# Recurrence chunks worked two heads at a time, and sparse scores as three 64-row products a head

## The chip, the cores and the metric

The kernel runs on one core of a Trainium2 chip, in one launch. The metric is the device time of that core in microseconds (us), the median of several executions. All arithmetic stands in the kernel; the host only lays out the arrays.

## What is computed

One forward pass of a model of two layer stacks over 512 tokens of width 1024, all in 32-bit floats. The first stack (two layers) is the one that matters here. Each of its layers projects the normed input and runs two token mixers side by side, then two dense stages:

```
S_t = diag(f_t) S_{t-1} + k_t v_t^T,  o_t = S_t^T q_t      # gated recurrence, 4 heads of 128, chunks of tokens
  A  = einsum('bhtd,bhsd,bhtsd->bhts', q, k, decay)        # within a chunk, decay = exp(b_t - b_s), b = cumsum(log f)
  o  = A v + (q * exp(b)) S                                # S: the state that the chunk begins with
sparse attention: 8 query heads of 64, 2 key heads
  s = q k^T * scale + mask,  p = softmax(s),  o = p v      # a "selected" and a "window" branch
  and a third branch over 31 compressed keys; three gates weigh the branches
```

With 512 tokens every block is selected, so the selected and the window branch are two causal attentions with their own keys. The second stack (two layers with retention, convolution, cross attention and a dense feed-forward) is not touched by the change.

## The kernel before

Activations lie feature by token, 128 features (partitions, "rows") by 512 tokens. A 32-bit operand x is split for TensorE into a high part xh (type fp32r, one pass) and a rest xl, and a product w·x is taken as wh·xh + wh·xl + wl·xh: three one-pass products. A product whose operands stay plain fp32 is issued as two instructions (x2 in the trace), but for transposes, which are one.

A scheduler orders the instructions of each engine after the program has been written out; each engine then runs its own queue in that order. PSUM tiles of the tag `xb` share six banks, taken in turn: a new one waits until the bank of the sixth before it has been read out. Tiles of the tag `a` share 41 slots.

**The recurrence, `hgrn_mix`.** 512 tokens are 4 chunks of 128; with 4 heads that is 16 units (c, h) a layer. `levels` makes, for one head, eight cumulated sums of log f by four products with constant 0/1 matrices (`lm`, into two banks `pn`), takes their exponentials on ScalarE (ACT, tiles `E`), and multiplies them on VectorE (DVE) with k and q (tile `kq`): seven levels that halve the chunk, of spans 64, 32, 16, 8, 4, 2 and 1. GpSimd (POOL) makes q·exp(b) (`qb`) in three steps, DVE the decay of the whole chunk (`ebl`). `scores` takes one product for each level (bank `pa`, line L1041; for spans 64 and 32 three small ones on 64 and 32 of the array's columns, L1044) and one for the last level and the diagonal (bank `pb`, L1045), and puts A together: the diagonal by DVE (L1046), spans 64 and 32 by three copies on ACT (L1049), the others by five predicated copies on DVE (L1053). `chunk_out` applies A and the state (`po`, `pd`).

**The fill.** Between the units `pump` issues half a projection each time (12 or 24 products `lin_...`, L463 to L465, of 128 x 512), from `first_fill`, which also rotates and splits the queries: `stacked` puts the high part of a head's 64 rows and, in the other 64 rows of the same tile, its rest (two ACT and two DVE instructions of 64 rows for one tile, two tiles for a pair of heads).

**The sparse scores, `nsa_pairs`.** 24 units a layer: 4 pairs of heads j, query tiles t = 3, 2, 1, 0 (n = 128(t+1) keys), both branches together for t = 1 and 0. `probs` takes for each head hd of the pair one product over 128 rows, (q high; q rest) with (k high; k high) (L1299, tile `kh` holds the keys twice), one over the head's 64 rows, q high with k rest (L1300, `kl`), then the causal mask (L1303), and the softmax on DVE and ACT. `values`, two units later, turns the weights (`pt`, L1339) and multiplies them with v (`no`, L1352): products that use 64 of the array's columns, the two heads of a pair on either half. The compressed branch closes a pair j with a product over 128 rows (L1356) and one over 64 rows (L1357).

Of the kernel before, what the change touches and what calls it, by code (L numbers as in the profile page):

```python
# [8 lines left out]
FT = mybir.dt.float32  # L9
# [161 lines left out]
def consts():  # L171
    c = {}
# [20 lines left out]
    c["lmask"] = mk.reshape(128, -1)  # L193
# [30 lines left out]
CWIDTH = dict(ident=128, causal=128, cmask=256, lm=768, lt=256, lmask=448, blk2=2,  # L224
# [115 lines left out]
class Kern:  # L340
# [44 lines left out]
    NSLOT = 41  # L385
# [365 lines left out]
    def first_fill(self, l, xs, gate):  # L751
# [8 lines left out]
        self.kh = self.ap.tile([128, 2, 2, 512], FR, name="kh", tag="kh", bufs=1)  # L760
        self.kl = self.ap.tile([128, 2, 512], FR, name="kl", tag="kl", bufs=1)
# [10 lines left out]
        def norm_out(i):  # L772
# [6 lines left out]
            for hd, (a, b) in enumerate((HALVES, HALVES[::-1])):  # L779
                nc.scalar.activation(self.kh[a, hd, i], k[a], AF.Copy)  # L780
                nc.scalar.activation(self.kh[b, hd, i], k[a], AF.Copy)
                nc.vector.tensor_tensor(self.kl[a, i], k[a], self.kh[a, hd, i].bitcast(FT), op=OP.subtract)
# [186 lines left out]
    def hgrn_mix(self, l):  # L969
# [3 lines left out]
        lmask = self.c["lmask"].rearrange("p (l t) -> p l t", l=7)  # L973
        self.O = []
# [8 lines left out]
        def chunk_in(c):  # L983
            lf = lfs.pop(c)
            kt = self.kt[c]
            kq = self.ap.tile([128, 4, 320], FT, name="kq", tag="kq", bufs=2)
            pk = self.xbank("pk")
            for h in range(4):
                s = slice(h * 128, (h + 1) * 128)
                nc.gpsimd.tensor_copy(kq[:, h, 128:256], self.hq[h][:, c * 128:(c + 1) * 128])  # L990
                nc.tensor.transpose(pk[:, s], kt[:, s], self.ident)
            nc.scalar.activation(kq[:, :, :128], pk.rearrange("p (h t) -> p h t", h=4), AF.Copy)
# [10 lines left out]
        def levels(c, h):  # L1003
            lf, kq, kd, ebl, A, qb = cs[c]
            s = slice(h * 128, (h + 1) * 128)
            Es = [self.slot("E") for _ in range(2)]
            for half in range(2):
                pn = self.xbank("pn")
                for g in range(2):
                    o = (g + half * 2) * 256 - (half and g) * 256  # L1010
                    mm(pn.rearrange("p (l g i) -> p g l i", l=4, g=2)[:, g], lhsT=lf[g][:, s], rhs=lm[:, o:o + 256],
                       start=True, stop=True)
                n = 512 - 32 * half
                nc.scalar.activation(Es[half][:, :n], pn[:, :n], AF.Exp)

            nc.vector.tensor_tensor(ebl[:, h:h + 1], Es[1][:, 319:320], Es[1][:, 383:384], op=OP.mult)
            for i, hs in enumerate(LEVELS[:-1]):
                z = Es[i // 4][:, i % 4 * 128:i % 4 * 128 + 128].rearrange("p (b u i) -> p b u i", u=2, i=hs)
                b0 = kq[:, h, :]
                src = bass.AP(tensor=b0.tensor, offset=b0.offset,  # L1020
                              ap=[list(b0.ap[0]), [2 * hs, 64 // hs], [128 + hs, 2], [1, hs]])
                nc.vector.tensor_tensor(z, z, src, op=OP.mult)
            odd = lambda a: a.rearrange("p (b u) -> p b u", u=2)[:, :, 1]
            half = lambda a: a.rearrange("p (g i) -> p g i", g=2)
            nc.vector.tensor_tensor(half(kq[:, h, 256:]), half(Es[1][:, 384:512])[:, :, :32], half(odd(kq[:, h, 128:256])), op=OP.mult)
            b = h * 128
            nc.gpsimd.tensor_tensor(qb[:, b:b + 64], Es[1][:, 256:320], kq[:, h, 128:192], op=OP.mult)
# [841 lines left out]
```

## Time and profile before

| | us |
|---|---|
| median of 3 runs | 2724.56 (2722.22 to 2724.98) |
| profiled execution, its own time | 2727.17 |
| its span, first to last instruction | 2725.4 |

The profile is one execution. TensorE (PE) is busy 99% of its span, VectorE 57%, ScalarE 42%, GpSimd 19%; the granted clock is 0.996 of full. [...] What a product costs is read from the time between its start and the start of the next; weight loads (PEld) run beside. In layer 0 the chunks of the recurrence run from 108 to 222 us and the sparse units from 222 to 390 us; in layer 1 from 576 to 694 and from 694 to 862 us. Of layer 1 the trace shows nearly the same pattern as of layer 0.

### The profile page before, as it was taken

The numbers are of one execution on the slowest core, as the hardware profiler recorded it, in microseconds if no ns is written. First come the engines' busy times: TensorE is split into PE (matmuls) and PEld (weight loads), VectorE is DVE, ScalarE is ACT, GpSimd is POOL, SyncE is SP. The second block draws the span as 40 slices with busy tenths as digits, with TensorE's granted clock in tenths as the row PEclk, the third lists the DMA queues.
The fourth block names the chain that finished last, engine by engine and source line by source line (L and its number), as shares of the span: only waits on it lengthen the run. The fifth ranks groups of instructions, "written<-read, shape, count | busy, mean of one in ns | idle before, by whom it ended". The sixth has DMA issues, their size and how long they took to land.

```text
span 2725.4 us, 34768 instructions
## 1 busy us (share of the span) xinstructions
PE 2686.5 (99%) x13510; PEld 2198.0 (81%) x13510; DVE 1546.8 (57%) x2561; ACT 1156.3 (42%) x2021; POOL 514.3 (19%) x488
## 2 busy tenths in 40 slices
PE   9999999999999999999999999999999999999998
PEld 7887678888767888888888888888888888888887
DVE  6686546787654655555555534455555555544444
ACT  5555654475565533333444322243333344422223
POOL 1263321035322141110101101014111000110001
PEclk9999999999999999999999999999999999999999
DMA  4311023321112332334322332332232441333332
GB/s 167 102 40 40 32 63 101 94 93 32 40 39 77 101 93 86 101 96 129 124 62 90 96 101 93 100 102 92 85 102 95 124 130 55 94 100 93 97 96 92
DMA packets 71747, 241.56 MB, mean 89 GB/s; under 512 B 8480, under 2 KB 11808, under 8 KB 71584
## 3 DMA queue, kind: packets, MB, share of 16 engines
q1 hardware_dynamic: 70144, 234.63, 27.6%
q0 software_dynamic: 1440, 4.72, 0.5%
q8 instruction: 107, 1.75, 0.3%
q14 instruction: 56, 0.46, 0.1%
HBM read 237.22 MB, written 2.10 MB: 88 GB/s over the span
## 4 chain that ended last, share of the span: by engine, by line
PE 67%; ACT 1%; DVE 1%; POOL 0%; issue 0%; DVEq 0%; ACTq 0%; POOLq 0%
PE lin_w L464 9%; PE lin_w L463 9%; PE lin_w L465 9%; PE lin_wy L463 1%; PE lin_xq L464 1%; PE lin_ga L465 1%; PE lin_xq L463 1%; PE lin_wo L464 1%; PE lin_wy L465 1%; PE lin_xq L465 1%; PE lin_gc L465 1%; PE lin_gb L465 1%; PE lin_wy L464 1%; PE lin_ga L464 1%; PE lin_ga L463 1%; PE lin_wo L463 1%
## 5 line engine op out<-in xcount | busy, mean ns | idle before, releaser
L425 ACT ACTIVATE whi<-wraw 128x1024 fp32r<-128x1024 f32 (+2 forms) x433 | 453.1, 1047 | 1112.2 <-issue 534.1
L427 DVE TENSOR_TENSOR wlo<-wraw,whi 128x1024 fp32r<-128x1024 f32 (+2 forms) x409 | 563.8, 1379 | 172.0 <-ACT whi L425 168.6
L465 PE MATMUL lin_w<-xh,wlo 128*128 128x512 f32 x704 | 273.9, 389 | 0.0
L464 PE MATMUL lin_w<-xl,whi 128*128 128x512 f32 x704 | 273.9, 389 | 0.0
L463 PE MATMUL lin_w<-xh,whi 128*128 128x512 f32 x704 | 273.9, 389 | 0.0
L1489 POOL TENSOR_TENSOR fa<-fa,fb 128x512 f32<-128x512 f32 x44 | 60.3, 1370 | 614.6 <-DVE fb L610 482.8
L463 PEld LDWEIGHTS lin_w<-xh,whi 128*128 128x128 f32 x704 | 132.2, 188 | 27.6
L465 PEld LDWEIGHTS lin_w<-xh,wlo 128*128 128x128 f32 x704 | 132.2, 188 | 27.5
L464 PEld LDWEIGHTS lin_w<-xl,whi 128*128 128x128 f32 x704 | 132.2, 188 | 27.3
L464 PE MATMUL lin_w<-fyl,whi 128*128 128x512 f32 (+1 forms) x366 | 139.9, 382 | 0.9 <-DVE fyl L511 0.9
L463 PE MATMUL lin_w<-fyh,whi 128*128 128x512 f32 (+1 forms) x366 | 139.6, 381 | 0.0
L465 PE MATMUL lin_w<-fyh,wlo 128*128 128x512 f32 (+1 forms) x366 | 139.5, 381 | 0.0
L610 DVE TENSOR_TENSOR fb<-lin_w,rs 128x512 f32<-128x512 f32 x44 | 30.4, 691 | 138.9 <-PE lin_w L465 138.9
L568 POOL TENSOR_TENSOR nacc<-sq 128x512 f32<-128x512 f32 x11 | 16.5, 1500 | 456.0 <-ACT sq L562 408.5
L1314 ACT ACTIVATE P<-S,nm,qkst 128x512 f32<-128x512 f32 (+3 forms) x128 | 77.4, 610 | 52.5 <-DVE nm L1309 39.4
L1307 DVE TENSOR_REDUCE nm<-S 128x1 f32<-128x512 f32 (+3 forms) x96 | 56.2, 598 | 61.9 <-PE S L1303 61.5
L1499 DVE TENSOR_TENSOR h<-lin_w,h 128x512 f32<-128x512 f32 x40 | 27.7, 692 | 106.9 <-PE lin_w L465 106.9
L427 POOL TENSOR_TENSOR wlo<-wraw,whi 128x1024 fp32r<-128x1024 f32 x24 | 57.1, 2378 | 140.8 <-ACT whi L425 119.7
L1448 POOL TENSOR_TENSOR ga<-ga,gb 128x512 f32<-128x512 f32 x16 | 20.7, 1291 | 323.6 <-DVE gb L1447 323.6
L464 PEld LDWEIGHTS lin_w<-fyl,whi 128*128 128x128 f32 x366 | 68.8, 188 | 15.2 <-DVE fyl L511 2.2
L463 PEld LDWEIGHTS lin_w<-fyh,whi 128*128 128x128 f32 x366 | 68.8, 188 | 13.7 <-ACT fyh L510 0.2
L465 PEld LDWEIGHTS lin_w<-fyh,wlo 128*128 128x128 f32 x366 | 68.8, 188 | 13.0
(603 smaller groups left out, 6985.4 us busy)
## 6 DMA issues: line engine op xcount, KB each, us to landing
wraw<-in_w SPq DMA_DIRECT2D x396, 512.0 KB, 3.5
wraw<-in_w SPq DMA_DIRECT2D x34, 448.0 KB, 3.2
wraw<-in_w SPq DMA_DIRECT2D x8, 256.0 KB, 5.4
mem<-in_mem POOLq DMA_DIRECT2D x8, 256.0 KB, 4.0
out<-y SPq DMA_DIRECT2D x8, 256.0 KB, 2.2
h<-in_x SPq DMA_DIRECT2D x7, 256.0 KB, 5.5
wraw<-in_w SPq DMA_DIRECT2D x4, 420.0 KB, 3.0
pin<-in_p POOLq DMA_DIRECT2D x4, 256.0 KB, 3.0
```

The costliest lines, as they stand in the source:

```text
L425: self.nc.scalar.activation(h[:, c], t[:, c], AF.Copy)
L427: eng.tensor_tensor(lo[:, c], t[:, c], h[:, c].bitcast(FT), op=OP.subtract)
L463: mm(ps[:, :n], lhsT=wh[:, k, :], rhs=xh[:, :n], start=a, stop=False)
L464: mm(ps[:, :n], lhsT=wh[:, k, :], rhs=xl[:, :n], start=False, stop=False)
L465: mm(ps[:, :n], lhsT=wl[:, k, :], rhs=xh[:, :n], start=False, stop=b)
L568: eng.tensor_tensor(acc[:, :n], self.nacc[:, :n], sq[:, :n], op=OP.add)
L610: self.nc.vector.tensor_tensor(t, ps, rs, op=OP.mult)
L1307: nc.vector.tensor_reduce(nm[:, :nb, hd], Ss[hd][:, :nb * n].rearrange("p (u s) -> p u s", u=nb), axis=AX, op=OP.max, negate=True)
L1314: nc.scalar.activation(P[:, c], Ss[hd][:, c], AF.Exp, scale=rq[:, hd:hd + 1], bias=nm[:, i, hd:hd + 1], accum_out=sm[:, i, hd:hd + 1])
L1448: nc.gpsimd.tensor_tensor(gs[0], gs[0], gs[1], op=OP.add)
L1489: nc.gpsimd.tensor_tensor(a, a, b, op=OP.mult)
L1499: nc.vector.tensor_tensor(self.h[m], ps, self.h[m], op=OP.add)
```

## The change

- `hgrn_mix` works on units (c, p) of two heads. `levels(c, p)` fills four tiles `E`, each with two levels of both heads, so that one DVE instruction serves a level of both. A third product a head, with a matrix of ones (`ones_r`, 64 columns), adds the first half's sum to the second half's within the same bank, so that one exponential gives exp(b) for the whole chunk; `ebl` becomes a copy, `qb` one product, both on POOL.
- `scores(c, p)` takes every level by one product over all rows and columns; spans 64 and 32 go to a third bank `pg`. A is put together for both heads at once (constant `lmask` is doubled).
- The order around a unit is levels of the next, half a projection, `chunk_out`, scores, half a projection.
- Queries are split by `split` (one ACT, one DVE instruction on 128 rows), keys are held once. `probs` takes three products a head, all over its 64 rows: high·high, rest·high, high·rest, the two heads in turn. The rest of the compressed values is padded with zeros to 128 rows, so that its product uses all rows.

```diff
-            for hd in range(2):
-                hs, x = HALVES[hd], self.q1[j][hd]
-                o = Ss[hd][:, :nb * n].rearrange("p (b s) -> p b s", b=nb)
-                mm(o, lhsT=x[:, ts], rhs=self.kh[:, hd, bb, :n], start=True, stop=False)
-                mm(o, lhsT=x[hs, ts], rhs=self.kl[hs, bb, :n], start=False, stop=False)
...
+            for i, (x, k) in enumerate(((qh, self.kh), (ql, self.kh), (qh, self.kl))):
+                for o, hs in zip(os, HALVES):
+                    mm(o, lhsT=x[hs, ts], rhs=k[hs, bb, :n], start=i == 0, stop=False)
...
-                self.q1.append(self.stacked(rs[i], "q1"))
+                self.q1.append(self.split(rs[i], "q1"))
...
-                r, (vh, vl) = HALVES[j % 2], self.vc
-                mm(po[0], lhsT=vh, rhs=self.pc[j], start=False, stop=False)
-                mm(po[0], lhsT=vl[r, :], rhs=self.pc[j][r, :], start=False, stop=True)
+                mm(po[0], lhsT=self.vc[0], rhs=self.pc[j], start=False, stop=False)
+                mm(po[0], lhsT=self.vc[1 + j % 2], rhs=self.pc[j], start=False, stop=True)
...
+                for h in range(2):
+                    s = slice((2 * p + h) * 128, (2 * p + h) * 128 + 128)
+                    pn = self.xbank("pn")
+                    for g in range(2):
+                        o = (g + half * 2) * 256 - (half and g) * 256
+                        mm(pn.rearrange("p (l g i) -> p g l i", l=4, g=2)[:, g], lhsT=lf[g][:, s], rhs=lm[:, o:o + 256],
+                           start=True, stop=not (half and g))
+                    if half:
+                        mm(pn[:, 320:384], lhsT=lf[0][:, s], rhs=self.ones_r[:, :64], start=False, stop=True)
...
+            pa, pb, pc = self.xbank("pa"), self.xbank("pb"), self.xbank("pg")
+            at = lambda i: (pc, i * 128) if i < 2 else (pa, (i - 2) * 128)
+            for h in range(2):
+                for i, hs in enumerate(LEVELS[:-1]):
+                    t, o = at(i)
+                    E = Es[i // 2][:, i % 2, h]
+                    mm(t[:, o + h * 64:o + h * 64 + 64], lhsT=E, rhs=second(E, hs), start=True, stop=True)
...
-            if i < 15:
+            if i < 7:
                 E[i + 1] = levels(*units[i + 1])
-            if h == 0 and c:
+            self.pump(self.HPUMP[2 * i])
+            if p == 0 and c:
                 S = chunk_out(c - 1, S)
-            scores(c, h, E.pop(i))
-            self.pump(self.HPUMP[i])
+            scores(c, p, E.pop(i))
+            self.pump(self.HPUMP[2 * i + 1])
```

The scheduler orders the changed program anew. On PE, the first sparse unit of layer 0 (t = 3, one branch; S with its two numbers is the score bank of the first and of the second head) stood so before:

```order
L1299 MATMUL S_2297<-kh_1117,q1_1347 128x512
L1300 MATMUL S_2297<-kl_1118,q1_1347 128x512
L1299 MATMUL S_2298<-kh_1117,q1_1348 128x512
L1300 MATMUL S_2298<-kl_1118,q1_1348 128x512
L1303 LDWEIGHTS identb_203
L1303 MATMUL S_2297<-c_causal_229,identb_203 128x128
```

and stands so in the changed program:

```order
L1317 MATMUL S_2136<-kh_1133,q1h_1330 128x512
L1317 MATMUL S_2137<-kh_1133,q1h_1330 128x512
L1317 MATMUL S_2136<-kh_1133,q1l_1331 128x512
L1317 MATMUL S_2137<-kh_1133,q1l_1331 128x512
L1317 MATMUL S_2136<-kl_1134,q1h_1330 128x512
L1317 MATMUL S_2137<-kl_1134,q1h_1330 128x512
```

Four products that alternated between 128 and 64 rows have become six on 64 rows, first and second head in turn.

On PE, the last sparse unit of the first pair of heads (t = 0, both branches) stands so in the changed program, with products `no` of an earlier unit before and behind it:

```order
L1369 MATMUL no_2206<-PT_2389,vt_774 64x128
L1317 MATMUL S_2444<-kh_1133,q1h_1330 128x256
L1317 MATMUL S_2444<-kh_1133,q1l_1331 128x256
L1317 MATMUL S_2444<-kl_1134,q1h_1330 128x256
L1317 MATMUL S_2445<-kh_1133,q1h_1330 128x256
L1317 MATMUL S_2445<-kh_1133,q1l_1331 128x256
L1317 MATMUL S_2445<-kl_1134,q1h_1330 128x256
L1369 MATMUL no_2206<-PT_2395,vt_774 64x128
```

Here the scheduler has put the three of the first head ahead of the three of the second.

On PE, in chunk 1 of layer 0, one head of the recurrence with the fill behind it stood so before (`pa`, `pb` score banks, `lin_nq` the projection of the queries):

```order
L1044 MATMUL pa<-E 64x64
L1044 MATMUL pa<-E 32x32 x2
L1041 MATMUL pa<-E 128x64 x4
L1045 MATMUL pb<-kq 128x192
L463 MATMUL lin_nq_1577<-xh,whi 128x512
L464 MATMUL lin_nq_1577<-xl,whi 128x512
L465 MATMUL lin_nq_1577<-xh,wlo 128x512
L1011 MATMUL pn<-c_lm,lf 128x4x64 x4
```

and a pair of heads stands so now:

```order
L465 MATMUL lin_nq_1532<-xh,wlo 128x512
L1047 MATMUL pg<-E 128x64 x2
L1047 MATMUL pa<-E 128x64 x4
L1048 MATMUL pb<-kq 128x192
L1047 MATMUL pg<-E 128x64 x2
L1047 MATMUL pa<-E 128x64 x4
L1048 MATMUL pb<-kq 128x192
L463 MATMUL lin_nq_1532<-xh,whi 128x512
```

The products on 64 and 32 columns are gone, and the scores of two heads stand together, with 12 products of the fill ahead of them and 12 behind.

## Rows read from the trace of the kernel before

**Rows 1.** Timeline of PE, layer 0: start, length, line, tiles, shape, count.

```profile
319.77 0.50 PE L1299 MATMUL S<-kh,q 128*128 128x512 f32 x1
320.19 0.50 PE L1300 MATMUL S<-kl,q 64*128 64x512 f32 x1
320.62 0.39 PE L1303 MATMUL S<-c_causal,identb 128*128 128x256 bf16 x2
...
328.50 0.40 PE L465 MATMUL lin_hz<-xh,wlo 128*128 128x512 f32 x1
328.74 0.39 PE L1299 MATMUL S<-kh,q 128*128 128x512 f32 x1
329.05 0.49 PE L1300 MATMUL S<-kl,q 64*128 64x512 f32 x1
329.48 0.23 PE L1303 MATMUL S<-c_causal,identb 128*128 128x128 bf16 x1
```

**Rows 2.** Timeline of PE at the end of layer 0's sparse units.

```profile
386.35 0.39 PE L465 MATMUL lin_wout<-yh,wlo 128*128 128x512 f32 x1
386.67 1.53 PE L1352 MATMUL no<-PT,vt 128*64 128x128 f32 x24
388.13 0.50 PE L1356 MATMUL no<-pcs,vch 128*128 128x512 f32 x1
388.56 0.49 PE L1357 MATMUL no<-pcs,vcl 64*128 64x512 f32 x1
388.98 0.50 PE L463 MATMUL lin_wpp<-ph,whi 128*128 128x512 f32 x1
```

**Rows 3.** Timeline of PE in the retention of the second stack.

```profile
1019.86 0.82 PE L1592 MATMUL rsc<-rp 64*128 64x128 f32 x5
1020.42 0.37 PE L1607 MATMUL ro<-R,qx 64*128 64x128 f32 x1
...
1020.63 0.27 PE L1607 MATMUL ro<-R,qx 64*128 64x128 f32 x1
1020.64 0.27 PE L1592 MATMUL rsc<-rp 64*128 64x128 f32 x1
1020.74 0.27 PE L1607 MATMUL ro<-R,qx 64*128 64x128 f32 x1
```

**Rows 4.** Timeline of PE: the scores of one head of the recurrence.

```profile
152.44 0.40 PE L465 MATMUL lin_nq<-xh,wlo 128*128 128x512 f32 x1
152.76 0.51 PE L1044 MATMUL pa<-E 128*64 128x64 f32 x6
153.20 1.11 PE L1041 MATMUL pa<-E 128*128 128x64 f32 x8
154.15 0.54 PE L1045 MATMUL pb<-kq 128*128 128x192 f32 x2
```

**Rows 5.** Waits of PE, whole kernel: us in total, times, longest.

```profile
PE pa L1044 <- DVE E L1022: 6.2, 6, 1.6
PE pa L1044 <- DVE A L1053: 5.8, 6, 1.6
PE pt L1339 <- DVE P L1324: 3.5, 2, 1.8
```

**Rows 6.** DVE, groups by form, whole kernel: count, busy us, mean ns.

```profile
L1022 DVE TENSOR_TENSOR E<-E,kq 128x128 f32<-128x128 f32 x192 | 63.8, 370 | 4.4 <-ACT E L1014 4.3
L1053 DVE COPY_PREDICATED A<-c_lmask,pa 128x64 f32<-128x64 uint8 x128 | 30.7, 240 | 7.4 <-ACT A L1049 6.1
L1262 DVE TENSOR_TENSOR Pc<-Pc,cnm 128x256 f32<-128x256 f32 x8 | 3.3, 417 | 0.0
```

**Rows 7.** Stretches: length; busy PE, PEld, DVE, ACT, POOL; granted clock; DMA share; GB/s.

```profile
159.16:162.57 3.41, 3.41 (x10) 2.64 (x9) 1.87 (x11) 0.22 (x1) 1.36 (x5) 0.50 0.02 5
599.48:602.89 3.41, 3.41 (x13) 3.12 (x12) 2.89 (x17) 0.48 (x3) 2.33 (x8) 0.50 0.00 0
613.13:619.95 6.82, 6.82 (x28) 5.93 (x27) 2.94 (x14) 3.55 (x16) 1.38 (x4) 0.50 0.00 0
```

More of the change, by code (lines that the diff above doesn't have):

```diff
@@ L758, in first_fill @@
         self.rq = st
-        self.kh = self.ap.tile([128, 2, 2, 512], FR, name="kh", tag="kh", bufs=1)
-        self.kl = self.ap.tile([128, 2, 512], FR, name="kl", tag="kl", bufs=1)
+        self.kh, self.kl = [self.ap.tile([128, 2, 512], FR, name="k" + x, tag="k" + x, bufs=1) for x in "hl"]
         def norm_in(i):
@@ L1001, in chunk_in, with levels @@
             cs[c] = (lf, kq, kd, self.small([128, 4], "ebl", bufs=2), self.slot("A"), self.slot("qb"))
-        def levels(c, h):
+        def levels(c, p):
             lf, kq, kd, ebl, A, qb = cs[c]
-            s = slice(h * 128, (h + 1) * 128)
-            Es = [self.slot("E") for _ in range(2)]
+            Es = [self.slot("E").rearrange("p (l h t) -> p l h t", l=2, h=2) for _ in range(4)]
             for half in range(2):
[L1008 to L1027, printed above, removed]
-            nc.gpsimd.tensor_scalar(qb[:, b + 64:b + 128], Es[1][:, 320:384], Es[1][:, 319:320], None, op0=OP.mult)
-            nc.gpsimd.tensor_tensor(qb[:, b + 64:b + 128], qb[:, b + 64:b + 128], kq[:, h, 192:256], op=OP.mult)
@@ new lines, in levels @@
+                for h in range(2):
[7 more added lines that the diff above has]
+                        mm(pn[:, 320:384], lhsT=lf[0][:, s], rhs=self.ones_r[:, :64], start=False, stop=True)
+                    for k in range(2):
+                        nc.scalar.activation(Es[half * 2 + k][:, :, h], pn[:, k * 256:k * 256 + 256].rearrange("p (l t) -> p l t", l=2),
+                                             AF.Exp)
@@ new lines, in levels @@
+                for i, hs in list(enumerate(LEVELS[:-1]))[half * 4:half * 4 + 4]:
+                    z = Es[i // 2][:, i % 2].rearrange("p h (b u i) -> p (h b) u i", u=2, i=hs)
+                    b0 = kq[:, p, :]
+                    src = bass.AP(tensor=b0.tensor, offset=b0.offset,
+                                  ap=[list(b0.ap[0]), [2 * hs, 128 // hs], [Q0 + hs, 2], [1, hs]])
+                    nc.vector.tensor_tensor(z, z, src, op=OP.mult)
+            cum, odd = Es[3][:, 0], Es[3][:, 1]
@@ new lines, in scores @@
+            f = lambda x, hs: x.rearrange("p (b i) -> p b i", i=hs)
+            for i, hs in list(enumerate(LEVELS))[2:-1]:
+                nc.vector.copy_predicated(second(a, hs), f(lmask[:, i], hs), f(pa[:, (i - 2) * 128:(i - 1) * 128], hs))
+            b0 = pb[:, :]
+            src = bass.AP(tensor=b0.tensor, offset=b0.offset, ap=[list(b0.ap[0]), [320, 2], [1, 64]])
+            nc.vector.copy_predicated(a.rearrange("p (h b u) -> p h b u", h=2, u=2)[:, :, :, 1],
+                                      lmask[:, 6].rearrange("p (h t) -> p h t", h=2), src)
@@ L1078, in chunk_out @@
             return Sn
-        units = [(c, h) for c in range(4) for h in range(4)]
+        units = [(c, p) for c in range(4) for p in range(2)]
         chunk_split(0)
@@ L1084, in hgrn_mix @@
         S = None
[L1085 to L1086 removed]
+        for i, (c, p) in enumerate(units):
+            if p == 0 and c < 3:
                 chunk_split(c + 1)
[L1088 removed]
+            if p == 1 and c < 3:
                 chunk_in(c + 1)
[L1090 removed]
+            if i < 7:
                 E[i + 1] = levels(*units[i + 1])
[L1092 removed]
+            self.pump(self.HPUMP[2 * i])
+            if p == 0 and c:
                 S = chunk_out(c - 1, S)
[L1094 to L1095 removed]
+            scores(c, p, E.pop(i))
+            self.pump(self.HPUMP[2 * i + 1])
         chunk_out(3, S)
@@ L1205, in compress @@
             vc = self.small([128, 128], "vc", bufs=1)
-            self.vc = [self.small([128, 128], "vc" + x, dt=FR, bufs=1) for x in "hl"]
+            self.vc = [self.small([128, 128], "vc" + x, dt=FR, bufs=1) for x in "hab"]
             nc.gpsimd.memset(vc, 0.0)
+            for x, r in zip(self.vc[1:], HALVES[::-1]):
+                nc.gpsimd.memset(x[r].bitcast(FT), 0.0)
             for i in range(4):
```

69 lines of the change are left out of this document (34 added, 35 removed).

## The prediction

> **What bounds the kernel now.** I read the page first: PE is never free for long, no transfer shows among its waits, so time is what PE's queue takes plus PE's waits. Then the timeline of PE, from start to start. A one-pass product of 512 columns follows another on 128 rows after 0.23 to 0.24 us [rows 1]. The reader is to see what happens where the tile of the array changes, to 64 rows or to 64 or 32 columns. The product over 64 rows, L1300, keeps the next one waiting 0.43 us, and a 128-row L1299 between two of them 0.42 [rows 1]; a first L1299, entered from a 128-row product, takes 0.31. So a change of tile costs 0.09 ahead of it and about 0.10 behind it: 0.195 in all. For the products `no` on 64 columns it is a little less: entry 0.32 instead of 0.23, and 24 instructions, 12 pairs, take 1.46 where 12 x 0.11 are 1.32 [rows 2]; that is 0.09 + 0.14 for entering and leaving, and some of the 0.20 by which the next product is late, which it shares with the change behind it. I take 0.145 a change.
>
> Then the waits: in the chunks of the recurrence PE waited 6.2 us for the products E of DVE and 5.8 us for a bank that DVE's predicated copies still read [rows 5]; at the start of the sparse units 3.5 us, 1.8 a layer, for the first softmax [rows 5]. Last the clock: it was granted at half, 1.2 of 2.4 GHz, in three stretches, 13.6 us in all [rows 7], all within the chunks of the recurrence.
>
> **Do two 64-row products overlap?** That is what the change rests on, since three products of 64 rows replace one of 128 and one of 64. The sparse part shows no such pair, but retention does: five L1592 on one half of the rows take 0.56, 0.11 each, and where L1592 and L1607 lie on different halves, a second one starts 0.01 after the first and the next such pair 0.11 after that [rows 3]. Two cost what one costs, weight loads of 128 columns included. Bounds for a pair of 512 columns: 0.23, if it does the same, and 0.46, if one-pass products run one after another; I take 0.23, the row's own behaviour. A rule of the Trainium skill says less: "TensorE: Matmul & The Clock Gate", section "Measured speedup vs the span model", gives 3.07 times for four row tiles of 512 columns; an estimate from it is 0.30 for a pair, and by it the saving below would be about 5.5 us smaller, 2712. No pair in retention shows such a loss, but those are of 128 columns.
>
> **The change, part by part.** Both layers together; the counts are from the two programs' orders.
>
> 1. Products of the scores. Before 192, one after another: 96 of 512 columns at 0.23, 64 of 384 at 0.175, 32 of 256 at 0.12 (shares of 0.23 by columns, not under 0.11): 37.1 us. Now 288. The scheduler leaves two heads side by side in 88 pairs (44, 38, 6) and 112 products alone (56, 20, 36), as in the second piece of order shown: 100 x 0.23 + 58 x 0.175 + 42 x 0.12 = 38.2. **+1.1**.
> 2. Changes of tile around them: 192 before, 156 now, and not fewer, because the scheduler puts `no` and fill between the heads of many units. 36 x 0.195 = **-7.0**.
> 3. Changes around `no`: 158 before, 122 now: 36 x 0.145 = **-5.2**.
> 4. The compressed values: L1356 takes 0.43, L1357 0.42 and the product behind it 0.34 [rows 2]; without a change of tile 0.33 + 0.23 + 0.23. 0.40 x 8 = **-3.2**.
> 5. Small level products: per head 0.09 on the product ahead, 0.44 for L1044, 0.05 on L1041 (0.95 for 8 where 8 x 0.112 are 0.90) [rows 4]; now four instructions of 0.112. 0.13 x 32 = **-4.2**. 96 changes of tile go with them.
> 6. The product with ones: 64 columns, one pass; its cost lies between 0.03 (64 of 512 columns) and 0.12 (one L1041). With 128 weight columns to load I take 0.11: x 32 = **+3.5**.
>
> PE's own queue: -15.0 us.
>
> 7. Waits in the chunks. DVE's work for a pair of heads falls: products from 12 x 0.370 to 6 x 0.417 (a row of that size), predicated copies from 8 x 0.240 to 4 at a price between 0.24 and 0.48, 0.30 taken, as doubled products grow little [rows 6]: 6.4 to 3.7 us, 42 us over 16 pairs. E of a pair is also ready a whole unit ahead of its scores. That speaks for the 6.2 us to go. The 5.8 us need not: a pair takes seven banks of six, so the next pair's `pn` wait for the copies out of `pa`, with only 12 products of fill, 2.8 us, between. The chain there is 0.42 + 4 x 0.30 on DVE and three short copies on ACT; 1.2 us are left for those and whatever DVE had queued. Bounds: all 12 us gone, or as much again as now (+12). I take **-6**.
> 8. The start of the sparse units. The first turned weights stand behind 14 products of fill, not 30, and behind scores that are 2 us shorter, while the softmax starts only 0.7 us earlier. The bound is 16 x 0.23 = 3.7 us a layer, and nothing if ACT, which ran exponentials behind a weight split, comes earlier now. **+3** for both.
> 9. At nothing: splits of queries and keys (fewer, larger instructions on DVE and ACT, neither at the end of a wait outside 7 and 8); the exponentials, now eight of 256 instead of four of 512, ready a unit ahead (if not, their wait is E's in 7); POOL's `qb` (three steps become one); one more constant load ahead of the first weights. The clock: 0, between -6.8 (never half) and +6.8 (twice as long).
>
> Sum: -15.0 - 6 + 3 = **-18.0 us**. The profiled execution took 2727.2, 2.6 above the median; the same difference off the median 2724.6 is **2707**.
>
> **Rivals.**
> - *More comes*: all chunk waits go, the first softmax is in time, and more than half of the half clock (-4) goes with the waits: -15 - 12 - 4 = -31, 2694. For it speaks DVE's relief; against it the banks. 0.13.
> - *The softmax chain takes back half*: parts 1 to 4 save 14.3 us, and a unit of scores is then shorter than what DVE and ACT do for it wherever no fill stands between; 7 us back: 2714. 0.12.
> - *Pairs overlap in part*, being one-pass products of up to 512 columns: the overlap is worth 44 x 0.23 + 38 x 0.175 + 6 x 0.12 = 17.5 us; a quarter to a half of it lost is 2711 to 2716. 0.07. The figure of the page named above lies in there.
> - *Not at all*: 2725, no change, and the scores' part would not do what it says. Retention's pairs speak against it [rows 3]. 0.05.
> - *Slower: the pair's copies hold the banks.* If DVE lags by over 1.8 us at each of 16 pairs, `pn` waits 29 us instead of 12 for E and A, and 2724.6 - 15 + 17 + 3 is 2730. The longest wait now is 1.6 [rows 5]; below that price the change is not slower. 0.05.
> - The forecast: 0.58, its own range 2698 to 2715.
>
> **How the numbers follow.** About 0.2%, 5.4 us, can be told from no change here. Faster: forecast, more, half taken back, and overlap in part: 0.90, less 0.03 for their tails above 2719, 0.87. Same: no overlap and those tails, 0.08. Slower: the banks, 0.05. The range runs from "more" to beyond overlap in part, 2692 to 2720; it leaves out no overlap and the slower case, 0.10, and some of the tails.
>
> **What would show it.** In the changed profile: L1317 of two heads start 0.01 apart and the next two 0.23 later; if 0.23 lies between the two, part 1 is wrong. Two padded products close each pair of heads with 0.23 between. No product stands on 64 or 32 columns in the chunks, and an L1017 takes 0.11. Waits for E are gone; waits of `pn` or `pg` for A tell part 7, those of `pt` for P part 8. A half clock for longer than 13.6 us would speak for clumps of small products. The forecast fails if waits in the chunks exceed 20 us, or if pairs do not overlap.

## The result and the profile after

| | before | after |
|---|---|---|
| median, us | 2724.36 (2722.22 to 2724.98, 4 runs) | 2696.28 (2693.26 to 2697.41, 4 runs) |
| profiled execution, its span | 2727.17, 2725.4 | 2693.26, 2691.5 |

The ratio is 0.9893, 95% interval 0.988 to 0.9905: 28.1 us less, where 18.0 were forecast. The profiled execution of the changed kernel is its fastest, 3.0 below the median, that of before 2.8 above its own, so the two traces differ by 33.9.

The timeline of PE where the sparse units of layer 0 begin (start, length, line, tiles, shape, count) answers to [rows 1]:

```profile
211.54 0.50 PE L1317 MATMUL S<-kh,q1h 64*128 64x512 f32 x2
211.88 0.40 PE L1317 MATMUL S<-kh,q1l 64*128 64x512 f32 x2
212.12 0.40 PE L1317 MATMUL S<-kl,q1h 64*128 64x512 f32 x2
212.45 0.29 PE L1319 MATMUL S<-c_causal,identb 128*128 128x128 bf16 x2
...
212.67 0.50 PE L1317 MATMUL S<-kh,q1h 64*128 64x512 f32 x2
```

Each row holds the two heads. Two pairs follow each other after 0.24, as one product did; a change of tile ahead adds 0.10 (0.34), one behind 0.09 (0.33). A unit of both heads takes 1.13. The compressed values answer to [rows 2], without a change of tile between them and behind them, 0.34 + 0.23:

```profile
371.14 1.53 PE L1369 MATMUL no<-PT,vt 128*64 128x128 f32 x24
372.60 0.50 PE L1372 MATMUL no<-pcs,vch 128*128 128x512 f32 x1
372.94 0.40 PE L1373 MATMUL no<-pcs,vcb 128*128 128x512 f32 x1
373.17 0.39 PE L463 MATMUL lin_wpp<-ph,whi 128*128 128x512 f32 x1
```

The scores in the recurrence, answering to [rows 4], all on the full array; eight L1047 take 0.90, and the fill behind starts without a gap:

```profile
152.27 0.55 PE L1047 MATMUL pg<-E 128*128 128x64 f32 x4
152.66 1.06 PE L1047 MATMUL pa<-E 128*128 128x64 f32 x8
153.56 0.54 PE L1048 MATMUL pb<-kq 128*128 128x192 f32 x2
153.81 0.53 PE L463 MATMUL lin_nq<-xh,whi 128*128 128x512 f32 x1
```

The waits of PE over the whole kernel (us in total, times, longest). Those of [rows 5] for E and A are gone without a successor in the chunks; what is left lies at the start and near the end of the sparse units:

```profile
PE pt L1356 <- DVE sm L1335: 4.6, 2, 2.3
PE S L1317 <- ACT P L1331: 3.2, 2, 1.6
PE no L1369 <- ACT PT L1360: 1.6, 2, 0.8
```

The groups of DVE by form (count, busy us, mean ns), answering to [rows 6]; a doubled copy takes 335 on average, its median is 299:

```profile
L1026 DVE TENSOR_TENSOR E<-E,kq 128x256 f32<-128x256 f32 x96 | 68.1, 773 | 4.6 <-ACT E L1019 4.2
L1060 DVE COPY_PREDICATED A<-c_lmask,pa 128x128 f32<-128x128 uint8 x64 | 21.4, 335 | 10.9 <-ACT A L1057 9.3
```

The mean of 773 for a product on two heads mixes two cases. The shortest, the median and the longest of these products, of the kernel before and of the changed one:

```profile
L1022 DVE TENSOR_TENSOR E<-E,kq x192: 273/280/1361, 113.5 to 682.1; 128x128 f32<-128x128 f32 x192
L1026 DVE TENSOR_TENSOR E<-E,kq x96: 409/465/1511, 113.5 to 643.3; 128x256 f32<-128x256 f32 x96
```

Where POOL runs nothing beside it, a product on two heads takes 0.41 us (30 of the 96), the forecast's 0.417, and one on a single head 0.28, not 0.370. The other 66 overlap an instruction of POOL and take 0.94 on average; 44 of them take over 0.6, before it was 16 of 192. So DVE's products of E, 63.8 us before, take 68.1 now. One beside POOL's `qb`, and five alone behind it:

```profile
140.32 0.72 POOL L1030 TENSOR_TENSOR qb<-E,kq 128x256 f32<-128x256 f32 x1
140.33 1.00 DVE L1026 TENSOR_TENSOR E<-E,kq 128x256 f32<-128x256 f32 x1
...
141.25 1.75 DVE L1026 TENSOR_TENSOR E<-E,kq 128x256 f32<-128x256 f32 x5
```

The stretches at half clock before the last instructions (length; busy PE, PEld, DVE, ACT, POOL; granted clock), answering to [rows 7]. Half as long as before, they moved from the chunks to the sparse units:

```profile
344.90:348.31 3.41, 3.41 (x17) 2.09 (x17) 2.05 (x8) 3.05 (x12) 0.00 (x0) 0.50 0.00 0
798.87:802.28 3.41, 3.41 (x19) 2.42 (x19) 2.08 (x10) 3.06 (x12) 0.00 (x0) 0.50 0.74 237
```

The first begins 0.3 us after a wait of PE of 1.6 us, at a unit of 256 columns:

```profile
344.60 0.38 PE L1317 MATMUL S<-kh,q1h 64*128 64x256 f32 x1 [1.61 <-ACT P L1331]
```

These stretches belong to single executions. The kernel before ran 15 times beside e1, at 2723.2 to 2729.0 us and granted clocks of 0.998 to 0.996, 0.997 in the median; the four executions of the changed kernel have 0.996 to 0.998, 0.997 in the median too. The trace of before stands at 0.996, that of the changed kernel at 0.998. So the difference of the clock between the two traces is no more than executions of one kernel differ by, and the medians show none to a thousandth, some 3 us.

**Where the time went.** For each layer, "chunks" is the time from the first L991 to the first product of the sparse scores, "sparse" from there to the last product of the compressed values. Everything outside these two stages is the same within 1 us. Each stage is split: the waits that PE's view lists in it, what its half-clock stretches cost (half their length: products that follow each other after 0.23 do so after 0.43 there, as e2 below shows), and the rest, PE's queue. Both layers together, us, in the one traced execution of each kernel (the half-clock columns give the stretches' length):

| | chunks | waits | half clock | queue | sparse | waits | half clock | queue |
|---|---|---|---|---|---|---|---|---|
| before | 231.2 | 13.6 | 13.7 | 210.8 | 332.6 | 7.0 | 0 | 325.6 |
| after | 207.6 | 0 | 0 | 207.6 | 322.8 | 9.4 | 6.8 | 310.0 |

The chunks gave 23.6 us: 13.6 of waits, 6.8 of clock, 3.2 of queue. The sparse units gave 9.8: 15.6 of queue, of which waits took back 2.4 and the clock 3.4. Without the clock that is 18.8 of queue and 11.2 of waits, 30.0, near the 28.1 of the medians.

### The profile page after: what moved, and what is told of

It reads as the page before. It is cut to its first block, busy times and chain, and to the rows that moved or that the text cites. A ratio compares the mean times of both kernels' runs of the same rounds, so it can differ in the third digit from the quotient of the medians.

```text
span 2691.5 us, 34626 instructions
## 1 busy us (share of the span) xinstructions
PE 2663.3 (99%) x13574; PEld 2199.9 (82%) x13574; DVE 1534.0 (57%) x2310; ACT 1142.1 (42%) x2017; POOL 499.0 (19%) x430
## 3 DMA queue, kind: packets, MB, share of 16 engines
q1 hardware_dynamic: 70288, 234.86, 28.1%
## 5 line engine op out<-in xcount | busy, mean ns | idle before, releaser
L463 PEld LDWEIGHTS lin_w<-fyh,whi 128*128 128x128 f32 x366 | 68.8, 188 | 13.7
```

What stands on the lines that cost most here:

```text
L463: mm(ps[:, :n], lhsT=wh[:, k, :], rhs=xh[:, :n], start=a, stop=False)
```

## The experiments

The theory that the runs were to test: the queue of PE does what the forecast priced; the surplus is waits and clock in the chunks, and these went because E of a pair of heads is ready a whole pair ahead of its scores. The rivals: they went because DVE has less to do; or because of what the sparse part leaves behind; and for the sparse units, that only the changes of tile paid and the halves of the array do not really run beside each other. Each run is compared with runs of the kernel before on its own chip; these had medians of 2726.2 (e1 to e4), 2729.4 (e5 to e8), 2727.8 (e9 to e11) and 2726.3 us (e12), so runs of different groups are compared by their ratios, not by their times. The stages, waits and stretches are of one traced execution of each.

| run | median us | ratio to before, 95% | chunks | waits | half clock | sparse | waits | half clock |
|---|---|---|---|---|---|---|---|---|
| e1_sparse_only | 2716.3 | 0.9965 (0.9952 to 0.9977) | 228.8 | 9.3 | 17.1 | 325.9 | 9.5 | 13.7 |
| e2_chunks_only | 2724.8 | 0.9997 (0.9988 to 1.0006) | 211.5 | 2.7 | 0 | 349.0 | 17.0 | 10.2 |
| e3_per_head | 2696.5 | 0.9892 (0.9877 to 0.9907) | 207.6 | 0 | 0 | 323.3 | 9.5 | 3.4 |
| e4_kept_together | 2813.1 | 1.0319 (1.0305 to 1.0333) | 210.9 | 2.6 | 0 | 436.3 | 90.7 | 99.0 |
| e5_heads_apart | 2716.6 | 0.9960 (0.9946 to 0.9974) | 207.6 | 0 | 0 | 344.7 | 0 | 13.7 |
| e6_value_order | 2680.8 | 0.9830 (0.9817 to 0.9844) | 207.6 | 0 | 0 | 310.3 | 10.9 | 6.8 |
| e7_lead_two | 2704.4 | 0.9915 (0.9901 to 0.9928) | 215.2 | 5.2 | 0 | 324.3 | 9.4 | 10.2 |
| e8_full_levels | 2713.0 | 0.9944 (0.9932 to 0.9957) | 223.9 | 11.5 | 10.2 | 325.9 | 9.3 | 13.7 |
| e9_lead_full | 2707.8 | 0.9926 (0.9913 to 0.9938) | 220.3 | 8.3 | 13.7 | 324.1 | 9.4 | 10.2 |
| e10_first_pairs | 2681.7 | 0.9831 (0.9818 to 0.9844) | 207.6 | 0.2 | 0 | 310.5 | 13.9 | 6.8 |
| e11_early_fill | 2680.1 | 0.9827 (0.9814 to 0.9841) | 207.6 | 0.2 | 0 | 309.3 | 8.9 | 10.2 |
| e12_dve_per_head | 2699.6 | 0.9900 (0.9883 to 0.9916) | 211.0 | 2.8 | 0 | 326.1 | 9.4 | 13.7 |

Half-clock columns give the length of the stretches; they cost half of it.

### e1_sparse_only and e2_chunks_only: the two parts alone

e1 is the kernel before with the parts of the diff shown ahead for keys, queries, compressed values and `nsa_pairs`; e2 has the others, those of `hgrn_mix` and its constant, with one slot of the tag `a` less. Of the lines below e1 has the old form throughout, e2 only in the last two:

```diff
-        units = [(c, h) for c in range(4) for h in range(4)]
+        units = [(c, p) for c in range(4) for p in range(2)]
...
-    NSLOT = 41
+    NSLOT = 42
```

> The kernel before with the sparse scores alone changed: queries split once, three products of 64 rows for each head, compressed values padded to full rows; the chunks stay as they were. If the forecast's parts 1 to 4 and 8 are right (1.1 - 7.0 - 5.2 - 3.2 + 3), 11.3 us go and it takes 2713. The two traces say 9.8 us less from the first score to the last product of the attention, 2714.6. If part of what the chunks gained came from the sparse change (the state in which it leaves banks or clock), it ends below 2708; if the row pairs cost more than they save outside the changed kernel, at 2724.

> The kernel before with the chunks alone changed (two heads at a time, product with ones), the sparse scores as before. By the forecast's parts 5 to 7 (-4.2 + 3.5 - 6) 6.7 us go: 2717.7. By the traces the chunks of both layers are 23.7 us shorter, and if that belongs to this change alone it takes 2701. If the two changes do not add up (11 from the sparse part, and this one well above 2705), the gain of the chunks needs both.

Alone, the sparse part gives 9.9 us (forecast 11.3) and the chunks 1.4, nothing that can be told from zero; together they give 28. Two losses make the difference. The first lies in e2. Its chunks are 19.7 us shorter than before, but the old sparse units behind them are 16.4 us longer: 10.0 more waits and 5.1 of clock. PE's waits in e2:

```profile
PE no L1367 <- DVE PT L1360: 7.8, 4, 2.5
PE pt L1354 <- DVE P L1339: 6.1, 2, 3.1
```

and the longest single one, the first softmax, in the timeline of e2:

```profile
224.25 2.34 POOL L427 TENSOR_TENSOR wlo<-wraw,whi 128x1024 fp32r<-128x1024 f32 x1
224.34 2.54 DVE L1339 TENSOR_SCALAR P<-P,sm 128x512 f32<-128x512 f32 x1
...
227.02 1.94 PE L1354 MATMUL pt<-c_ident,P 128*128 128x128 f32 x8 [3.06 <-DVE P L1339]
...
228.23 0.49 DVE L1339 TENSOR_SCALAR P<-P,sm 128x512 f32<-128x512 f32 x1
```

The scaling of the first weights starts 0.09 us behind a weight split on POOL and takes 2.54 us, over five times its 0.49 four us later; PE waits 3.06 for it. Late in that wait a stretch of 6.8 us at half clock begins, in which products of the fill follow each other after 0.42 instead of 0.23:

```profile
226.27:233.09 6.82, 6.07 (x19) 5.12 (x20) 4.50 (x11) 3.87 (x10) 1.50 (x2) 0.50 0.23 77
...
230.47 0.63 PE L463 MATMUL lin_nz<-xh,whi 128*128 128x512 f32 x1
230.89 0.63 PE L464 MATMUL lin_nz<-xl,whi 128*128 128x512 f32 x1
```

In the changed kernel the same meeting falls on the second head's weights, and PE lists no wait for them; but it waits 2.3 us a layer for the first head's all the same. So of the 7.6 us that e2 waits more in its sparse units than the changed kernel, only 1.5 lie here. The value products make 6.2 (7.8 against 1.6). The longest wait among them, too, comes behind a scaling that runs beside a weight split, with two more instructions of DVE ahead of the copy that PE waits for:

```profile
276.33 2.70 DVE L1339 TENSOR_SCALAR P<-P,sm 128x512 f32<-128x512 f32 x1
276.35 2.40 POOL L427 TENSOR_TENSOR wlo<-wraw,whi 128x1024 fp32r<-128x1024 f32 x1
...
281.68 0.43 PE L1367 MATMUL no<-PT,vt 128*64 128x128 f32 x2 [2.51 <-DVE PT L1360]
```

The second loss lies in e1: its five executions have a granted clock of 0.993 to 0.995, where before has 0.996 to 0.998 and the changed kernel too; 0.003 of 2716 us is 8 us, an estimate. So the parts don't add up because each alone has a loss that the whole has not, some 8 us of waits in e2 and of clock in e1. Why the splits meet other instructions in e2, and why e1's clock is lower, was not tested; nor was the one slot that e2 has less.

### e3_per_head and e5_heads_apart: do the halves of the array run side by side?

```diff
-            for i, (x, k) in enumerate(((qh, self.kh), (ql, self.kh), (qh, self.kl))):
-                for o, hs in zip(os, HALVES):
+            for o, hs in zip(os, HALVES):
+                for i, (x, k) in enumerate(((qh, self.kh), (ql, self.kh), (qh, self.kl))):
```

> The changed kernel with the six 64-row products of a unit written head by head, three and three, not in turns. The scheduler then leaves 36 products beside one of the other half instead of 88 (18, 14 and 4 of 512, 384 and 256 columns), with as many changes of tile (314). If a pair costs one product, 26 x 0.23 + 24 x 0.175 + 2 x 0.12 = 10.4 us come back: 2706.7. If products on the two halves run one after another and only the changes of tile paid, it stays at 2696.

No difference: 2696.5. Neither expectation's reason holds, and the trace shows why. PE's queue of e3 has the first unit so, three products of one head, then three of the other:

```
L1317 MATMUL S_2136<-kh_1133,q1h_1330 128x512
L1317 MATMUL S_2136<-kh_1133,q1l_1331 128x512
L1317 MATMUL S_2136<-kl_1134,q1h_1330 128x512
L1317 MATMUL S_2137<-kh_1133,q1h_1330 128x512
L1317 MATMUL S_2137<-kh_1133,q1l_1331 128x512
L1317 MATMUL S_2137<-kl_1134,q1h_1330 128x512
```

and its timeline shows them in pairs all the same, at the distances of the changed kernel:

```profile
212.09 0.51 PE L1317 MATMUL S<-kh,q1h 64*128 64x512 f32 x2
212.43 0.41 PE L1317 MATMUL S<-kh,q1l 64*128 64x512 f32 x2
212.67 0.40 PE L1317 MATMUL S<-kl,q1h 64*128 64x512 f32 x2
```

Here a half of the rows starts its next product, 0.01 us behind the other half's, without waiting for products ahead of it in the queue that use the other half; so PE keeps its queue's order only within a half. What counts is therefore not which product stands beside which, but the longer half of an unbroken run of 64-row products. By that count, over the two programs' orders, e3 should be 1.9 us longer than the changed kernel; its queue in the sparse units is 2.1 longer (312.1 against 310.0). e5 breaks each run with a 128-row product, the causal one, behind which the second head is queued:

```diff
-            for o in os:
-                mm(o[:, :, n - 128:], lhsT=self.identb, rhs=self.c["causal"][:, None, :].to_broadcast([128, nb, 128]),
...
+            for o, hs in zip(os, HALVES):
+                for i, (x, k) in enumerate(((qh, self.kh), (ql, self.kh), (qh, self.kl))):
...
+                        with self.tc.issue_after(last.ins):
+                            mm(o, lhsT=x[hs, ts], rhs=k[hs, bb, :n], start=i == 0, stop=False)
+                last = mm(o[:, :, n - 128:], lhsT=self.identb, rhs=self.c["causal"][:, None, :].to_broadcast([128, nb, 128]),
```

> The changed kernel with the causal product of the first head between the two heads' 64-row products: three, causal, three, causal. The same products, but no 64-row product has one of the other half next to it. Counted over the runs of 64-row products, the longer half of each run adds up to 36.3 us in the changed kernel and to 55.7 here; 68 more changes of tile at 0.195 are 13.3. If halves run beside each other in any order, as the third run suggests: 19.4 + 13.3 = 32.7 us more, 2729. If they never overlap and the gain of the sparse part was in the changes of tile alone: 13.3 more, 2709.

It takes 2716.6, between the two. Its timeline shows what the overlap is worth, since a head alone takes 1.07 where two take 1.13 above:

```profile
212.33 0.50 PE L1319 MATMUL S<-kh,q1h 64*128 64x512 f32 x1
212.67 0.40 PE L1319 MATMUL S<-kh,q1l 64*128 64x512 f32 x1
212.91 0.39 PE L1319 MATMUL S<-kl,q1h 64*128 64x512 f32 x1
213.24 0.23 PE L1323 MATMUL S<-c_causal,identb 128*128 128x128 bf16 x1
213.40 0.50 PE L1322 MATMUL S<-kh,q1h 64*128 64x512 f32 x1
```

PE's queue in the sparse units grows by 27.9 us (344.7 less 6.8 of clock, against 310.0), near the 32.7 of overlap and tiles and far from the 13.3 of tiles alone. The time grows by only 20 because the slower scores cover all waits of the stage, 9.4 us; the clock costs 3.4 more. The halves do overlap.

### e6_value_order: the price of a change of tile

```diff
-                    for hd in range(2):
+                    for hd in (1, 0):
                         v = self.vt[i][:, b * 128 + hd * 64:b * 128 + hd * 64 + 64]
```

> The changed kernel with one word of order: the two heads of a step of the value products in the order 1, 0. The first one then waits for the later of the two turned weights, and no single one is left ahead of the rest: 254 changes of tile instead of 314 in all; the 64-row products lie a little worse (38.3 us by the longer halves instead of 36.3). If a change costs what the forecast took: 60 x 0.145 to 60 x 0.195 less 2.0 is 6.7 to 9.7 us below the changed kernel, 2687 to 2690. If the changes of tile hide beside the waits of the softmax chain, no change: 2696. If the later start of the value products holds a bank, slower.

It takes 2680.8, 0.9830 of before: 14 us less queue than the changed kernel, well above the 6.7 to 9.7 expected. In the changed kernel 40 value products of 320 stand alone, as here, where the next one starts 0.36 later; inside a group two of them, one in each half of the columns, take some 0.21 together (the 24 rows at 371.14 above are twelve products, and take 1.46 with entering and leaving):

```profile
238.77 0.43 PE L1369 MATMUL no<-PT,vt 128*64 128x128 f32 x2
239.13 0.40 PE L1317 MATMUL S<-kh,q1h 64*128 64x256 f32 x2
```

(A value product is two rows of the trace.) A single one thus pays not only two changes of tile; it and the odd one left behind also lack a partner in the other columns, another 0.21. By the two programs' orders 38 singles are gone: an estimate of 60 x 0.145 + 38 x 0.21 - 2.0 = 14.7, near what was measured. This is the best kernel of the study, with the two that follow from it.

### e7_lead_two, e8_full_levels, e9_lead_full: what empties the chunks of waits

All three are e1 with the chunks still one head at a time. e7 makes E two heads ahead; e8 takes the levels 64 and 32 on the full array; e9 does both.

```diff
-        E = {0: levels(0, 0)}
+        E = {0: levels(0, 0), 1: levels(0, 1)}
...
-            if i < 15:
-                E[i + 1] = levels(*units[i + 1])
+            if i < 14:
+                E[i + 2] = levels(*units[i + 2])
```

```diff
-                if i > 1:
-                    mm(pa[:, i * 64:(i + 1) * 64], lhsT=E, rhs=second(E, hs), start=True, stop=True)
-                    continue
-                for a in range(0, 128, 2 * hs):
-                    mm(pa[a:a + hs, i * 64:i * 64 + hs], lhsT=E[:, a:a + hs], rhs=E[:, a + hs:a + 2 * hs], start=True, stop=True)
+                mm(pa[:, i * 64:(i + 1) * 64], lhsT=E, rhs=second(E, hs), start=True, stop=True)
```

> The first run's kernel (sparse part changed, chunks one head at a time as before; 2716.3) with E made two heads ahead of its scores instead of one. DVE's instructions, PE's products and tiles are the same. If the waits for E and for A in the chunks (4.8 and 3.9 us in the first run) went because a pair of heads has a longer lead, they go here too, and with them part of the half clock: 5 to 15 us less, 2701 to 2711. If they went because DVE was relieved or because a bank now serves two heads, 2716 with the waits in place.

> The first run's kernel (2716.3) with the products of the levels 64 and 32 as full ones, one head at a time: 96 changes of tile less in the chunks, nothing else moved. Forecast part 5: 0.13 x 32 = 4.2 us less, 2712. If these changes hide in PE's waits for DVE there: 2716; if shorter runs of PE also cost the clock in the chunks and that comes back: below 2710.

> The first run's kernel (sparse part changed, 2716.3) with both: E two heads ahead (11.9 us less alone) and the levels 64 and 32 as full products (3.3 less alone). The chunks still go one head at a time, without the product with ones. If lead and tiles are what the changed chunks gain, this comes within some 5 us of the changed kernel: 2716.3 - 11.9 - 3.3 = 2701, or less by the 2.1 us of the ones that it does not have, 2699. If two heads in one bank and in one instruction are worth more than that by themselves, it stays above 2705.

The lead alone, beside e1, gives 13.6 us by the ratios and by the length of the chunks (228.8 to 215.2), with not one instruction of DVE or PE changed. The waits of e1 in the chunks:

```profile
PE pa L1038 <- DVE E L1019: 2.8, 4, 0.9
PE po L1058 <- DVE A L1050: 2.3, 2, 1.1
PE pa L1041 <- DVE A L1050: 2.3, 2, 1.6
PE pa L1041 <- DVE E L1019: 2.0, 4, 0.6
```

and of e7:

```profile
PE po L1058 <- DVE A L1050: 2.0, 2, 1.3
PE pa L1041 <- DVE A L1050: 1.3, 1, 1.3
PE pa L1041 <- DVE E L1019: 1.1, 2, 0.6
```

The waits for E fall from 4.8 to 1.1, those for A from 4.6 to 3.3, and the 17.1 us at half clock are gone, 8.5 us of time: the larger part of what the lead gives. (Over all their executions the median granted clock is 0.994 in e1 and 0.9965 in e7, some 7 us.) e8 gives 4.9 us in the chunks, about the forecast's 4.2; by the ratios it is 5.7, with intervals that just overlap. PE's queue in the chunks is 3.7 shorter (e1: 228.8 - 9.3 - 8.5 = 211.0; e8: 223.9 - 11.5 - 5.1 = 207.3). e9 missed, and by more than its expectation shows, which took 11.9 and 3.3 us from times on different chips: the queue is shorter by both, 205.2, but PE now comes early to where A is assembled, waits there, and the clock falls again, 13.7 us of it:

```profile
PE po L1054 <- DVE A L1046: 3.4, 4, 1.6
...
PE pa L1037 <- DVE A L1046: 1.7, 1, 1.7
```

So lead and full tiles are not all: something else in the changed chunks also clears the waits for A. It may be the pairs, or the half projection that the changed order puts ahead of `chunk_out` and the scores; no run takes that away alone, and which it is stays open.

### e12_dve_per_head: is it DVE's relief?

The changed kernel with each of DVE's instructions on a pair written as two; for the level products (the copies, the diagonal and the last level likewise):

```diff
-                    z = Es[i // 2][:, i % 2].rearrange("p h (b u i) -> p (h b) u i", u=2, i=hs)
...
+                    for h in range(2):
+                        z = Es[i // 2][:, i % 2, h].rearrange("p (b u i) -> p b u i", u=2, i=hs)
...
+                        nc.vector.tensor_tensor(z, z, src, op=OP.mult)
```

> The changed kernel with each of DVE's instructions on a pair of heads in the chunks written as two, one for each head; PE's products, the lead of E, the banks and the rest as changed. DVE's work in the chunks of a layer, 84.7 us there, grows by 32 x (2 x 0.240 - 0.335) + 8 x (2 x 0.295 - 0.450) + 8 x (2 x 0.282 - 0.415) + 8 x (2 x 0.303 - 0.322) - (48 x 0.773 - 96 x 0.371) = 7.7 us, to 92 of 104. If the waits for E and A went because DVE has less to do (the forecast's reason in part 7), PE waits for A again, up to 0.7 us for each of 16 pairs, and it takes 2700 to 2708. If the longer lead and one bank for two heads do it alone, it stays at 2696 and PE waits for nothing in the chunks.

It takes 2699.6, just under the relief's range; by the intervals of the two ratios alone that is no clear difference, but the chunks are 3.4 us longer than the changed kernel's. Waits come back there, 2.8 us of the 13.6 of before, and no half clock:

```profile
PE pn L1013 <- DVE A L1065: 2.1, 4, 0.6
...
PE pa L1050 <- DVE E L1027: 0.8, 2, 0.4
```

What the joined instructions of DVE are worth is real, but it is the small part.

### e4_kept_together, e10_first_pairs, e11_early_fill: attempts at a better kernel

e4 puts the six products of a unit into one block that the scheduler doesn't break. e10 and e11 build on e6: e10 orders the last four products of a unit behind the first two (the diff's core below), e11 moves a step of fill from a late unit to behind the first (`APUMP` "101111111010011101101011", was "001111111010011101101111").

```diff
+            with self.tc.tile_critical():
                 for i, (x, k) in enumerate(((qh, self.kh), (ql, self.kh), (qh, self.kl))):
```

```diff
+                    if len(firsts) < 2:
+                        firsts.append(mm(o, lhsT=x[hs, ts], rhs=k[hs, bb, :n], start=i == 0, stop=False))
+                        continue
+                    with self.tc.issue_after(firsts[1].ins), self.tc.issue_after(firsts[0].ins):
+                        mm(o, lhsT=x[hs, ts], rhs=k[hs, bb, :n], start=i == 0, stop=False)
```

> The changed kernel with the six products of a unit as one block that the scheduler does not break: 144 pairs instead of 88 and none alone, 96 changes of tile around them instead of 156, but 168 around the value products instead of 122. By the forecast's prices: 28 x 0.23 + 10 x 0.175 + 18 x 0.12 = 10.4 us less for the pairs, 60 x 0.195 = 11.7 less and 46 x 0.145 = 6.7 more for the changes of tile: 15.4 us below the changed kernel, 2681. Rival: the block needs both banks free before its first product, and PE waits for the softmax of the unit before: no gain, 2696 to 2705, with new waits of the scores for DVE or ACT in the sparse units.

e4 is 117 us slower than the changed kernel. PE's queue in the sparse units does get 13.9 us shorter (436.3 - 90.7 - 49.5 = 296.1), near the 15.4 priced, but by the profile's releasers the block waits for work that no score needs, such as a weight's transfer (9.1 us in all) and POOL's compressed weights:

```profile
PE S L1318 <- POOL pcs L1296: 14.2, 2, 7.2
```

It prices the block, not the pairs. (The expectation counts pairs by neighbours; after e3 the right count is the longer half of each run, 27.8 us here and 36.3 in the changed kernel.)

> The sixth run's kernel (value products in the order 1, 0; 2680.8) with the last four 64-row products of a unit ordered behind the first two, so that no head's three go ahead of a bank that the other still waits for. Longer halves 32.3 us instead of 38.3, and 262 changes of tile instead of 254: 6.0 less and 8 x 0.195 = 1.6 more, 2676. If the first head's products are late for their softmax by it, waits for DVE or ACT in the sparse units grow and it is 2681 or slower.

> The sixth run's kernel (2680.8) with one step of fill, 12 products, taken from late in the attention to behind the first unit's scores, where PE waits in each layer for the first turned weights, for the eighth-level ones and for the value products (4.6 + 2.7 + 1.7 us for both layers). If fill covers them: 5 to 9 us less, with the two half-clock stretches there (3.4 us each) gone, 2670 to 2676. If the softmax chain is simply moved later by 2.8 us, the waits stay: 2681; if the late units then lack fill, waits come up there and it is slower.

In e11's expectation, the ones said to be of an eighth level are the compressed weights `ptc`. Both come out level with e6, within a microsecond. e10's queue is 2.8 us shorter than e6's, and its waits 3.0 longer (13.9 against 10.9): the rival. e11 covers the first weights (their wait falls from 4.6 to 1.2) and waits 3.9 us for scores near the end, where e6 waits 2.1: the fill was needed there too, as its second rival said. In sum it waits 2.0 us less than e6 and loses 1.7 more by the clock.

## Why the prediction was right, and where its terms were off

The side and the range were right; the size was 10 us too small, and the result lies close to the rival "more comes" (2694). Its main step happened, all chunk waits went; its two others did not show: the first softmax was late, as in the forecast, and the medians show no gain of the clock. PE's queue fell by 18.8 us (forecast 15.0) and the waits by 11.2 (forecast 3).

- **Parts 1 to 4**, the sparse queue: -14.3 forecast, -15.6 measured. Pairs overlap, which the whole rested on [rows 3]. The estimate of 0.30 us a pair, worked out from the Trainium skill, "TensorE: Matmul & The Clock Gate", section "Measured speedup vs the span model", and with it 2712, did not come: 0.24 for two as for one. That the sum came so near is partly luck, for the split was wrong. From each product's start to the next one's, waits and half clock taken off, both layers, the scores went from 71.0 to 53.2 us, 17.8 less, where parts 1 and 2 say 5.9. The value products went from 55.5 to 56.0, where part 3 took 5.2 off: fewer changes of tile, but as many single products without a partner (e6). (A change of tile falls to either side of a border, so this split is rough.) The 112 products "alone" were priced as alone; some of them overlap in the queue's order too (e3): 36.3 us by the longer halves, not 38.2. That explains 1.9 us; the rest of the scores' surplus was not traced. Part 4 came as priced.
- **Parts 5 and 6**: -4.2 + 3.5 forecast; -3.7 for the queue in e8, and the product with ones adds 1.07 us for 16 in layer 0, 0.067 each, where 0.11 was taken: about +2.1. The chunks' queue is 3.2 shorter; the other 1.6 were not traced.
- **Part 7** is the step that failed in size: 6 us of waits were expected to go, 13.6 went (1.6 of them at L1041 and `po`, which the forecast did not list). Its reasons were mixed. A longer lead of E was named and is the larger cause that was found (e7). DVE's relief was overestimated, though its prices, 0.417 and 0.30, hold where DVE is undisturbed (0.41, and 0.299 in the median): the 0.370 of before was a mean with POOL's disturbances in it, 0.28 without, and in the changed kernel 44 of 96 products take over 0.6 beside POOL, where it was 16 of 192, so that DVE's products of E take 68.1 us instead of 63.8. Joining instructions is worth some 3 us in the chunks all the same (e12). The fear that a pair takes seven banks of six did not come true in the changed kernel, where no `pn` waits for A, but it did in part in e2 and e12, by 2.7 and 2.1 us.
- **Part 8**: +3 forecast. The waits for the first turned weights grew by 1.1 us (3.5 to 4.6), all waits of the sparse units by 2.4.
- **Part 9**, the clock at nothing, holds in the medians, 0.997 for both kernels, and not in the two traces, where 13.7 us at half clock went from the chunks and 6.8 came in the sparse units, 3.4 us of time in all. The forecast saw the stretches in the chunks [rows 7] and did not tie them to the waits in the same place. In the fourteen traces the chunks with 8 us of waits or more had 10 to 17 us at half clock, those with up to 5.2 none. But sparse units with 9.3 to 9.5 us of waits had 3.4 to 13.7, e5 had 13.7 without a wait, and executions of the kernel before at 0.998 have no room for what its trace shows. So the waits do not settle the clock, and what does stays open.

Sum of what was measured: chunks -23.6, sparse -9.8, -33.4 of the traces' 33.9. That the whole is more than e1 and e2 together comes from e2's waits in the sparse units and e1's lower clock.

## What to carry to other kernels

Before a gain is put down to the clock, compare the granted clocks of all executions: one trace of a kernel can have twice the half clock of the next. A mean duration of an instruction may hide two cases; look at the shortest and the median before doubling it. Where an engine fed another through many small steps here, making the data a unit earlier was worth more (13.6 us, three lines) than making it with fewer instructions (some 3). Products on parts of the array should come in unbroken runs, with the work of the parts balanced, and an order of issue that leaves one of them single costs two changes of tile and its partner.

## What the runs showed of the hardware that was not expected

- Products on the two halves of the rows start out of their queue's order: three of one half, then three of the other, ran as three pairs, each pair's starts 0.01 apart and the last pair 0.24 behind the one before (e3). The Trainium skill says otherwise: "TensorE: Matmul & The Clock Gate", section "The mechanism", has matmuls start and end strictly in program order; the trace decides, and here they did not start so.
- DVE's scaling of 128x512, 0.49 us four us later, took 2.54 when it started 0.09 us behind a weight split of POOL of 2.34 us (e2, both layers). The Trainium skill, "SBUF — State Buffer", section "Who interferes with whom", says that where DVE works in a two-port mode, the one of the two engines that comes second at their shared port is held for the whole instruction of the first; the trace agrees here.
- DVE's products of E on two heads took 0.41 us with nothing on POOL beside them and 0.94 on average with something (30 and 66 of 96, changed kernel).
- The clock can fall without a wait that the profile lists: in e5, where PE waited for nothing in the sparse units, it was at half for 6.8 us in each layer; in layer 0 that began at 217.22, after 4.9 us in which 64-row and causal products ran one after another.
